# When the second layer's rotary tables, the norms' transposes and the state-space projection are issued: four changes of order in a three-block kernel

## The chip, the cores and the metric

The kernel runs on one core of one Trainium2 chip. A core has five engines that run side by side and wait for each other only by semaphores: TensorE (PE, matmuls; its weight loads are PEld), VectorE (DVE), ScalarE (ACT), GpSimd (POOL) and SyncE (SP, which here issues the transfers from memory). The metric is the device time of one execution in microseconds, the median over runs.

## What is computed

Two layers of a first block (sequence 256, width 1024, feed-forward width 4096), each with attention and pooling side by side and a feed-forward, and then a second block with a state-space branch, an attention branch and a feed-forward. All in float32. In a layer, w_in gives the columns for the pooling, for q, for k and v, and the gates; q and k are normalized per head and rotated (rope) before the attention.

```python
def hybrid_layer(x, mod, ...):
    shift1, scale1, gate1, shift2, scale2, gate2 = jnp.split(mod[:, None, :], 6, axis=-1)
    h = rms_norm(x, norm1) * (1.0 + scale1) + shift1
    proj = h @ w_in
    ...
    mix = jnp.concatenate([y_pool, y_nsa], axis=-1) @ w_out
    x = x + gate1 * mix
    h2 = rms_norm(x, norm2) * (1.0 + scale2) + shift2
    ff = jnp.square(jax.nn.relu(h2 @ w_ff1)) @ w_ff2
    return x + gate2 * ff

def second_block(x, ...):
    u = h @ w_in
    z, xbc, dt_f_raw, dt_b_raw, q, k, v, gate_logits = jnp.split(u, ...)
    y_ssd = ssd_branch(z, xbc, ...) @ w_proj_ssd
    y_att = attention_branch(q, k, v) @ w_proj_attn
    gates = jax.nn.sigmoid(gate_logits + b_gate).reshape(bsz, s, N_BRANCHES, D_MODEL)
    mix = (gates[:, :, 0] * y_ssd + gates[:, :, 1] * y_att) @ w_out
    h = layer_norm(alpha * h + mix, ln1_g, ln1_b)
    f = jnp.square(jax.nn.relu(h @ w_up)) @ w_down
    h = layer_norm(alpha * h + f, ln2_g, ln2_b)
```

## The kernel before

Every float32 product is done as three matmuls: each operand is split into a high part, rounded to a format that PE reads fast, and the low rest. For activations these are hh and hl (made by `split`: hh on ACT at L103, hl on DVE at L106), for weights wh and wl. A weight chunk (512 KB) arrives in wst by a transfer that SP issues, ACT copies it to wh (L144), DVE subtracts to get wl (L145), and PE runs its 6 to 24 matmuls at L89.

The 256 tokens are two halves, t = 0 and t = 1, of 128 rows each; x0 and x1 hold them. An RMS norm of a half (`rms`) squares and sums on ACT, forms the mean on DVE (ss, L665), takes the power -1/2 on POOL (L119), and scales on DVE (xn, L668). Then `to_fm` brings it to feature-major form: eight transposes on PE (L479, four into bank tr and four into bank pv), scale and shift (hf: L488 on DVE, L486 on ACT), and the split into hh and hl, which PE then reads. How far behind the norm the transposes are put into the program is a number of steps:

```python
later(TU["ln"], lambda: to_fm(t, xn, hi, lo, MC[l, q0 + 1], MC[l, q0]))
```

A step (`tick`) is one group of matmuls of the product that is running; `later(n, f)` calls f after n steps. `Plan.at(step, f)` puts f at a step of a layer's big projection. From the program in this order each engine gets its instructions, as far as a scheduler that looks ahead leaves them there; the order within an engine is fixed before the run.

A layer keeps rotary tables (tab, ctab: the norm's weights times cosine and sine), made by POOL. `fetch` issues the transfers of three band matrices for the pooling and four pieces of w1, and fills part of kk. The feed-forward goes through eight slices of 512 columns: up(c) into bank st, ReLU (fr, L411 on ACT; in the first two slices transposed back on PE at L416), the square (L398 on ACT, L399 on POOL, the rest frl on DVE at L400), and down(c) into the four acc banks. `between(c)` is called after down(c). After its last slice `done` starts the next norm, half by half (t = 1 first within a layer, t = 0 first into layer 1). Sums for the modulation (macc, DVE L573) are mixed in between.

In the second block `large2` runs one big projection column group by column group, its gates (sig, ACT L1439) last but one: each gate reads an acc bank. `proj_ssd` then takes the same four acc banks (ybk) for the product of the state-space output yT (yh, yl) with w_proj_ssd: per chunk k six matmuls for each bank. After w_out, `done_ln1` makes the LayerNorm of a half (xn, L1708) and its transposes.

Of the kernel before, what the change touches and what calls it, by code (L numbers as in the profile page):

```python
# [24 lines left out]
ALPHA = 2.0 ** 0.25  # L25

SZ = 1024
TU = dict(aheadq=4, nst=5, tabc=2, nw=9, nt2=23, raw=1, krest=2, qrest=4, pool2=1, c2=3, c3=1, c4=1, ln=3, uv='uv', pre=[1], nv=5, nv1=0, nv0=0, u0=19.5, du=0.7, ub=2, uc=4, c0=32.5, dc=0.1, w0=36, dw=0.5, comp=22, pool=27, dpool=2, cmpa=32, cmpb=34, dcmp=2, e1=1, e0=1, pta=2, ahead=3, modp=3, rf=0.95, r0=0, r0b=3, r1=0.8, r1b=1.2, rs=17, raw_=4, qrest_=6, u0_=19.5, du_=1.0, comp_=22, pool_=26, cmpa_=31, cmpb_=35, nv_=0, nv0_=0, w0_=32, dw_=0.8, order2='v0 qk0 qk1 qk2 v1 B C x0 z0 x1 z1 x2 z2 x3 z3 g2 g3 pa g0 g1 ps', fm0=148, dfm=9, dts=8, dcd=30, par0=10, par1=40, d0=50, dd=2, db=3, dc2=5, ss0=70, ds=5.6, scb=5, sx=3, sr=6, sg=3.5, sy=3.5, sn=8, mf0=5, modp1=99, rf1=0.5, pool2_=3, c3_=2, c4_=3, nv1_=2, dpool_=2, dcmp_=1, dc_=0.4, cap=4, ub_=2.5, c0_=32.5, pta_=4)
NST, NW = TU['nst'], TU['nw']
NT2, NT4, NS5 = TU['nt2'], 5, 20  # L30

# [30 lines left out]
def tile_two_blocks(ctx: ExitStack, tc: tile.TileContext, I, out, stop=None, dbg=None):  # L62
# [450 lines left out]
    g2 = {}  # L513
# [177 lines left out]
    def first_norm(xn, rows, hi, lo, c):  # L691
# [17 lines left out]
            V.tensor_scalar(hf[:, ks], bt[:, ks], m[:, 2 + k:3 + k], m[:, k:k + 1], op0=OP.mult, op1=OP.add)  # L709
        split(fl(hi[:, 2 * c:2 * c + 2]), fl(lo[:, 2 * c:2 * c + 2]), hf, A)  # L710

    def hybrid_layer(l, hilo, between, done):
        hi, lo = hilo
        g = lay[l]
        act = act_of(hi, lo)
        U = lambda n: TU[n + "_"] if l and n + "_" in TU else TU[n]


        tabs = {}
        tab = [t2([128, 2, 2, 2, 64], "tab") for _ in range(2)]  # L720
        ctab = s5([32, 2, 64], "ctab")

        def tables():
            for i, n in enumerate(("qn", "kns", "knw")):
                tb = tab[i // 2][:, i % 2]
                w = P(l, n)
                for t in range(2):
                    cs, sn = C("cos")[:, t * 32:(t + 1) * 32], C("sin")[:, t * 32:(t + 1) * 32]
                    for hf in range(2):
                        G.tensor_tensor(tb[:, t, 0, hf * 32:(hf + 1) * 32], w[:, hf * 32:(hf + 1) * 32], cs, op=OP.mult)  # L730
                    G.tensor_tensor(tb[:, t, 1, 32:], w[:, 0:32], sn, op=OP.mult)
                    G.tensor_tensor(tb[:, t, 1, :32], w[:, 32:64], sn, op=OP.mult)  # L732
                    G.tensor_scalar(tb[:, t, 1, :32], tb[:, t, 1, :32], -1.0, None, op0=OP.mult)
                tabs[n] = tb
            w = P(l, "kn0")[:32]
            for hf in range(2):
                G.tensor_tensor(ctab[:, 0, hf * 32:(hf + 1) * 32], w[:, hf * 32:(hf + 1) * 32], C("ccos")[:32], op=OP.mult)
            G.tensor_tensor(ctab[:, 1, 32:], w[:, 0:32], C("csin")[:32], op=OP.mult)
            G.tensor_tensor(ctab[:, 1, :32], w[:, 32:64], C("csin")[:32], op=OP.mult)
            G.tensor_scalar(ctab[:, 1, :32], ctab[:, 1, :32], -1.0, None, op0=OP.mult)  # L740
# [45 lines left out]
        def evac_k(t, ps):  # L786
            k = t2([128, 8, 64], "kS")
            A.activation(fl(k), ps, AF.Copy)
            kd = t2([128, 4, 2, 64], "kd")
            for i in range(2):  # L790
                src = ps[:, 384 * i:384 * i + 128].rearrange("p (a b) -> p a b", a=2)
                A.activation(kd[:, 2 * i:2 * i + 2], src[:, :, None, :].to_broadcast([128, 2, 2, 64]), AF.Copy)
            later(U("raw") + 2 * t, lambda: raw_kv(t, kd))
            kr, rk = head_norm(k[:, 2:6], 4)
            tmp = t2([128, 4, 64], "krt")
            for i, n in ((0, "kns"), (1, "knw")):
                rope(kr[:, 2 * i:2 * i + 2], k[:, 2 + 2 * i:4 + 2 * i], tabs[n][:, t], tmp[:, 2 * i:2 * i + 2],
                     rk[:, 2 * i:2 * i + 2], 2)
# [29 lines left out]
        def evac_q(t, ps):  # L828
            q = t2([128, 8, 64], "qS")
            A.activation(fl(q), ps, AF.Copy)  # L830
            sq, r = head_norm(q, 8)
            rqs[t] = small.tile([128, 2, 8], FT, name="rqs", bufs=2)
            V.tensor_scalar(rqs[t][:, 0], r, -0.125, None, op0=OP.mult)
            V.tensor_copy(rqs[t][:, 1], r)
            qr = t2([128, 4, 2, 64], "qr")
            tmp = t2([128, 8, 64], "qrt")
            tab = tabs["qn"][:, t]
            by_group = lambda a: a.rearrange("p (g h) d -> p h g d", g=2)
            V.tensor_tensor(qr, by_group(q), tab[:, 0][:, None, None, :].to_broadcast([128, 4, 2, 64]), op=OP.mult)
# [49 lines left out]
        def compress2(hid):  # L889
# [14 lines left out]
                for i in range(2):  # L904
                    V.tensor_tensor(krd[:, i:i + 1], o, rb, op=OP.mult)

            rope(kr, kc, ctab, sq, ss[:, 1:2], 1, last)
            hv = s5([128, 2, 4, 16], "chv")
            V.tensor_copy(hv[64:128], hid[64:128][:, :, None, :].to_broadcast([64, 2, 4, 16]))
            later(U("c3"), lambda: compress3(hv, krd))  # L910
# [188 lines left out]
        def start():  # L1099
# [4 lines left out]
            for c in range(4):  # L1104
# [15 lines left out]
                if c == TU["tabc"]:  # L1120
                    nc.sync.dma_start(cst[:, 256:], I["cst"][:, 256:])
                    load_par(0)
                    tables()
                if c == 2:
                    W.depth = TU["aheadq"]
            for n, ev in (("q", evac_q), ("k", evac_k)):
# [454 lines left out]
    def proj_ssd():  # L1581
# [120 lines left out]
    def done_ln1(t):  # L1702
# [139 lines left out]
```

## Time and profile before

| | |
|---|---|
| median of 3 runs | 1243.47 us (1239.06 to 1244.24) |
| the profiled execution's own time | 1244.79 us |
| its span | 1243.0 us |
| mean granted clock of PE | 0.984 |
| PE busy | 1188.5 us (96%) |
| DVE busy | 831.0 us (67%) |
| ACT busy | 628.9 us (51%) |
| POOL busy | 194.6 us (16%) |

The span is that of one execution taken by the profiler; the time beside it also holds what lies around it. PE is nearly always busy, so time can change where PE waits, or where its granted clock (1.00 is 2.4 GHz, 0.50 is 1.2 GHz; a mean over a stretch lies between) is under 1.00. Names as tr, xn or hl are tiles of the program; "x4" behind an instruction joins four that follow each other.

### The profile page before, as it was taken

The page shows a single profiled execution, that of the slowest core. Times are in us where ns is not written, and L with a number is a line of the kernel's source. Part 1 is how long each engine was busy: PE and PEld are TensorE (multiplying, and loading weights), DVE is VectorE, ACT ScalarE, POOL GpSimd, SP SyncE. Part 2 cuts the span into 40 slices and gives each one's busy share as a digit, 9 for nine tenths or more (in the row PEclk, how much of TensorE's full clock was granted, in tenths as well). Part 3 has the DMA queues.
Part 4 walks back from the last instruction along what each step waited for, and adds up shares of the span by engine and source line. Part 5 has one row for each costly group of instructions (what it writes and reads, how often), then busy time and mean ns, then how long its engine had stood idle before and what let it go on. Part 6 is the DMA issues. An engine that isn't in the chain of part 4 may idle for free.

```text
span 1243.0 us, 19309 instructions
## 1 busy us (share of the span) xinstructions
PE 1188.5 (96%) x7352; PEld 1023.4 (82%) x7352; DVE 831.0 (67%) x1357; ACT 628.9 (51%) x1102; POOL 194.6 (16%) x207
## 2 busy tenths in 40 slices
PE   5999999999998999999999999999999999899997
PEld 2566787999876788789988999888888898799896
DVE  2466478887767866875453745688899768744544
ACT  2335446445445654654443543567688544645440
POOL 0421011311316100121110000011122102301101
PEclk8899999999998999999999999999999999999999
DMA  8867548899877620776663556575386654666640
GB/s 283 308 228 232 179 149 286 270 321 330 271 258 249 207 78 28 255 250 191 187 187 106 183 183 222 152 204 170 102 242 218 239 167 128 211 205 185 187 135 35
DMA packets 101788, 249.21 MB, mean 200 GB/s; under 512 B 9784, under 2 KB 15036, under 8 KB 101695
## 3 DMA queue, kind: packets, MB, share of 16 engines
q1 hardware_dynamic: 100902, 247.11, 62.4%
q8 instruction: 58, 0.95, 0.3%
q10 hardware_dynamic: 792, 0.86, 0.2%
q14 instruction: 36, 0.29, 0.1%
HBM read 246.03 MB, written 1.11 MB: 199 GB/s over the span
## 4 chain that ended last, share of the span: by engine, by line
PE 60%; issue 7%; DVE 7%; DMA 5%; POOL 3%; ACT 2%; DVEq 0%; SPq 0%; ACTq 0%; POOLq 0%
PE acc L89 38%; PE st L89 16%; DMA wst<-in_w_ff_dram 3%; DVE wl L145 2%; PE pv L89 2%; PE tr L89 2%; ACT wh L144 1%; DVE macc L573 1%; DMA wst<-in_w_mod_dram 1%; POOL fr L399 1%; DMA R<-rows 1%; POOL tab L732 1%; DMA wst<-in_w_down_dram 0%; PE st L980 0%; DVE frl L400 0%
## 5 line engine op out<-in xcount | busy, mean ns | idle before, releaser
L145 DVE TENSOR_TENSOR wl<-wst,wh 128x1024 fp32r<-128x1024 f32 (+3 forms) x324 | 401.4, 1249 | 143.2 <-ACT wh L144 142.1
L144 ACT ACTIVATE wh<-wst 128x1024 fp32r<-128x1024 f32 (+3 forms) x324 | 334.8, 1048 | 280.0 <-PE acc L89 83.7
L89 PE MATMUL st<-hh,wl 128*128 128x256 f32 x576 | 163.0, 283 | 0.0
L89 PE MATMUL st<-hl,wh 128*128 128x256 f32 x576 | 163.0, 283 | 0.0
L89 PE MATMUL st<-hh,wh 128*128 128x256 f32 x576 | 163.0, 283 | 0.0
L89 PE MATMUL acc<-wh,frl 128*128 128x512 f32 x384 | 152.6, 397 | 8.3 <-DVE frl L400 8.2
L89 PE MATMUL acc<-wl,frh 128*128 128x512 f32 x384 | 151.3, 394 | 0.0
L89 PE MATMUL acc<-wh,frh 128*128 128x512 f32 x384 | 151.2, 394 | 0.0
L399 POOL TENSOR_TENSOR fr<-fr 128x512 f32<-128x512 f32 x48 | 66.0, 1375 | 402.7 <-ACT frh L398 357.6
L89 PEld LDWEIGHTS st<-hl,wh 128*128 128x128 f32 x576 | 110.5, 192 | 0.9
L89 PEld LDWEIGHTS st<-hh,wl 128*128 128x128 f32 x576 | 110.4, 192 | 0.9
L89 PEld LDWEIGHTS st<-hh,wh 128*128 128x128 f32 x576 | 110.5, 192 | 0.0
L89 PEld LDWEIGHTS acc<-wh,frl 128*128 128x128 f32 x384 | 73.2, 191 | 26.0 <-DVE frl L400 11.7
L89 PE MATMUL acc<-wh,hl 128*128 128x512 f32 (+3 forms) x224 | 89.1, 404 | 1.3 <-DVE hl L106 1.3
L89 PE MATMUL acc<-wl,hh 128*128 128x512 f32 (+3 forms) x224 | 87.6, 391 | 2.4 <-DVE wl L145 2.4
L89 PE MATMUL acc<-wh,hh 128*128 128x512 f32 (+3 forms) x224 | 87.1, 389 | 0.0
L89 PEld LDWEIGHTS acc<-wh,frh 128*128 128x128 f32 x384 | 72.9, 190 | 15.3
L89 PEld LDWEIGHTS acc<-wl,frh 128*128 128x128 f32 x384 | 73.2, 191 | 14.2
L89 PE MATMUL acc<-hh,wl 128*128 128x256 f32 x288 | 83.0, 288 | 0.4 <-DVE ym L1462 0.4
L89 PE MATMUL acc<-hl,wh 128*128 128x256 f32 x288 | 81.9, 284 | 0.0
L89 PE MATMUL acc<-hh,wh 128*128 128x256 f32 x288 | 81.4, 283 | 0.0
L573 DVE SCALAR_TENSOR_TENSOR macc<-wst,cact,macc 128x1024 f32<-128x1024 f32 x55 | 72.6, 1320 | 5.1 <-DMA wst<-in_w_mod_dram 4.9
(341 smaller groups left out, 2250.4 us busy)
## 6 DMA issues: line engine op xcount, KB each, us to landing
wst<-in_w_ff_dram SPq DMA_DIRECT2D x128, 512.0 KB, 4.5
wst<-in_w_mod_dram SPq DMA_DIRECT2D x96, 512.0 KB, 5.2
wst<-in_w_in_dram SPq DMA_DIRECT2D x76, 512.0 KB, 4.7
wst<-in_w_up_dram SPq DMA_DIRECT2D x32, 512.0 KB, 4.0
wst<-in_w_down_dram SPq DMA_DIRECT2D x32, 512.0 KB, 4.3
wst<-in_w_out_dram SPq DMA_DIRECT2D x24, 512.0 KB, 3.8
ww<-in_w_in_dram SPq DMA_DIRECT2D x16, 512.0 KB, 5.6
R<-rows SPq DMA_DIRECT2D x32, 256.0 KB, 5.7
```

The source lines that it names most:

```text
L89: T.matmul(o, l, r, start=start, stop=stop, skip_group_check=True)
L144: A.activation(h[:, :kc * n], st[:, :kc * n], AF.Copy)
L145: V.tensor_tensor(l[:, :kc * n], st[:, :kc * n], h[:, :kc * n], op=OP.subtract)
L399: G.tensor_tensor(r, r, r, op=OP.mult)
L573: V.scalar_tensor_tensor(acc, st, cact[:, k:k + 1], acc, op0=OP.mult, op1=OP.add)
L732: G.tensor_tensor(tb[:, t, 1, :32], w[:, 32:64], sn, op=OP.mult)
```

## The change

Four pieces. The tables of layer 1 are made in the feed-forward of layer 0 after down(5) instead of at the start of layer 1. `fetch` of layer 1 is put at step 5 of its plan instead of ahead of it. The transposes of the norms come 5 steps behind the norm instead of 3, and those of the second block's first LayerNorm 5 steps behind instead of at once. `proj_ssd` takes its first two chunks together: both on banks 0 and 1, then both on banks 2 and 3.

```diff
-TU = dict(aheadq=4, ... ln=3, ...)
+TU = dict(fet=5, aheadq=4, ... ln=5, ...)
...
+    rope_tables = {}
+
+    def make_tables(l):
+        tabs = {}
+        tab = [t2([128, 2, 2, 2, 64], "tab") for _ in range(2)]
+        ctab = s5([32, 2, 64], "ctab")
+        for i, n in enumerate(("qn", "kns", "knw")):
+            tb = tab[i // 2][:, i % 2]
+            w = P(l, n)
+            for t in range(2):
+                cs, sn = C("cos")[:, t * 32:(t + 1) * 32], C("sin")[:, t * 32:(t + 1) * 32]
+                for hf in range(2):
+                    G.tensor_tensor(tb[:, t, 0, hf * 32:(hf + 1) * 32], w[:, hf * 32:(hf + 1) * 32], cs, op=OP.mult)
+                G.tensor_tensor(tb[:, t, 1, 32:], w[:, 0:32], sn, op=OP.mult)
+                G.tensor_tensor(tb[:, t, 1, :32], w[:, 32:64], sn, op=OP.mult)
+                G.tensor_scalar(tb[:, t, 1, :32], tb[:, t, 1, :32], -1.0, None, op0=OP.mult)
+            tabs[n] = tb
...
+        rope_tables[l] = tabs, ctab
...
                     load_par(0)
-                    tables()
+                    make_tables(0)
...
+        plan = Plan()
         if l:
-            tables()
-            fetch()
-        plan = Plan()
+            plan.at(U("fet"), fetch)
...
     def between0(c):
         if c == 4:
             load_par(1)
+        if c == 5:
+            make_tables(1)
...
-        for k in range(12):
+
+        plan.until(("fm", 0))
+        kept = [W.next(True) for _ in range(2)]
+        for b in (0, 2):
+            for k in range(2):
+                for i in range(2):
+                    proj(kept[k], k, b + i)
+                if b:
+                    W.release(1)
+                tick()
+                yield
+        for k in range(2, 12):
             if k % 4 == 0:
                 plan.until(("fm", k // 4))
...
-        to_fm(t, xn, *hh, Q("ln1g"), Q("ln1b"))
+        later(TU["ln"], lambda: to_fm(t, xn, *hh, Q("ln1g"), Q("ln1b")))
```

The first place is POOL's order around the start of layer 1; ss is a norm's mean, fr the squares of the feed-forward, macc a modulation sum. Before, with rows of the tables left out in the middle:

```order
L566 MEMSET macc 128x1024 x3
L399 TENSOR_TENSOR fr<-fr 128x512 x4
L576 TENSOR_TENSOR macc<-macc,wst 128x1024
L119 TENSOR_TENSOR ss<-ss,half 128x1
L730 TENSOR_TENSOR tab<-par,cst 128x32 x2
L731 TENSOR_TENSOR tab<-par,cst 128x32
L732 TENSOR_TENSOR tab<-par,cst 128x32
...
L733 TENSOR_SCALAR tab<-tab 128x32 x2
L119 TENSOR_TENSOR ss<-ss,half 128x1
L119 TENSOR_TENSOR hr<-hss,half 128x8
```

After:

```order
L566 MEMSET macc 128x1024 x3
L399 TENSOR_TENSOR fr<-fr 128x512 x2
L725 TENSOR_TENSOR tab<-par,cst 128x32 x2
L726 TENSOR_TENSOR tab<-par,cst 128x32
L727 TENSOR_TENSOR tab<-par,cst 128x32
...
L728 TENSOR_SCALAR tab<-tab 128x32 x2
L399 TENSOR_TENSOR fr<-fr 128x512 x2
L576 TENSOR_TENSOR macc<-macc,wst 128x1024
L119 TENSOR_TENSOR ss<-ss,half 128x1 x2
L119 TENSOR_TENSOR hr<-hss,half 128x8
```

The thirty instructions on tab stand between the squares of two slices, and the powers of both halves' norms follow each other.

The second place is DVE's order at the start of layer 0's feed-forward, from the norm of the first of its halves to the split that PE waits for (x_91 is half 0, x_92 half 1). Before:

```order
L668 TENSOR_SCALAR xn<-x_92,ss 128x512 x2
L145 TENSOR_TENSOR wl<-wst,wh 128x1024 x2
L488 TENSOR_SCALAR hf<-tr,mcol 128x128 x4
L1072 TENSOR_TENSOR rtmp<-acc,mgate 128x512
L106 TENSOR_TENSOR hl<-hf,hh 128x4x128 x2
L1073 TENSOR_TENSOR x_91<-x_91,rtmp 128x512
L1072 TENSOR_TENSOR rtmp<-acc,mgate 128x512
L145 TENSOR_TENSOR wl<-wst,wh 128x1024
L1073 TENSOR_TENSOR x_91<-x_91,rtmp 128x512
```

After:

```order
L668 TENSOR_SCALAR xn<-x_92,ss 128x512 x2
L145 TENSOR_TENSOR wl<-wst,wh 128x1024 x2
L1074 TENSOR_TENSOR rtmp<-acc,mgate 128x512
L488 TENSOR_SCALAR hf<-tr,mcol 128x128
L1075 TENSOR_TENSOR x_91<-x_91,rtmp 128x512
L488 TENSOR_SCALAR hf<-tr,mcol 128x128 x3
L145 TENSOR_TENSOR wl<-wst,wh 128x1024
L106 TENSOR_TENSOR hl<-hf,hh 128x4x128 x2
L1074 TENSOR_TENSOR rtmp<-acc,mgate 128x512
L145 TENSOR_TENSOR wl<-wst,wh 128x1024
```

Between xn and the hl of this half there are now also an update of x and a third weight split.

The third place is PE's order in the state-space projection; acc_9439 to acc_9442 are its banks 0 to 3, wh_9315 and wl_9316 chunk 0, wh_9360 and wl_9361 chunk 1. Before:

```order
L89 MATMUL acc_9440<-yh_9260,wl_9316 128x256
L89 MATMUL acc_9440<-yl_9261,wh_9315 128x256
L89 MATMUL acc_9440<-yh_9260,wh_9315 128x256
L1568 MATMUL tr_9477<-cst_75,yg_8251 128x128 x4
L89 MATMUL acc_9439<-yh_9260,wl_9361 128x256
L89 MATMUL acc_9439<-yl_9261,wh_9360 128x256
L89 MATMUL acc_9439<-yh_9260,wh_9360 128x256
L89 MATMUL acc_9441<-yh_9260,wl_9316 128x256
L89 MATMUL acc_9441<-yl_9261,wh_9315 128x256
L89 MATMUL acc_9441<-yh_9260,wh_9315 128x256
L89 MATMUL acc_9441<-yh_9260,wl_9316 128x256
```

After:

```order
L89 MATMUL acc_9440<-yh_9260,wl_9361 128x256
L89 MATMUL acc_9440<-yl_9261,wh_9360 128x256
L89 MATMUL acc_9440<-yh_9260,wh_9360 128x256
L89 MATMUL acc_9440<-yh_9260,wl_9361 128x256
L89 MATMUL acc_9440<-yl_9261,wh_9360 128x256
L89 MATMUL acc_9440<-yh_9260,wh_9360 128x256
L1571 MATMUL tr_9477<-cst_75,yg_8251 128x128 x4
L89 MATMUL acc_9441<-yh_9260,wl_9316 128x256
L89 MATMUL acc_9441<-yl_9261,wh_9315 128x256
L89 MATMUL acc_9441<-yh_9260,wh_9315 128x256
L89 MATMUL acc_9441<-yh_9260,wl_9316 128x256
L89 MATMUL acc_9441<-yl_9261,wh_9315 128x256
```

Before, 15 matmuls stand ahead of the first one on bank 2 (twelve of chunk 0, three of chunk 1); now 24 do.

## Rows read from the trace of the kernel before

**Rows 1.** the page's part 1: busy time, share of the span and instructions

```profile
PE 1188.5 (96%) x7352; PEld 1023.4 (82%) x7352; DVE 831.0 (67%) x1357; ACT 628.9 (51%) x1102; POOL 194.6 (16%) x207
```

**Rows 2.** waits of PE: what ended them, us in total, times, longest

```profile
PE tr L479 <- DVE xn L1708: 2.5, 2, 2.1
...
PE tr L848 <- DVE qr L843: 1.5, 1, 1.5
```

**Rows 3.** timeline, start of layer 1: start, us, instruction, [idle before <- what ended it]

```profile
376.54 0.63 PE L479 MATMUL tr<-cst,xn 128*128 128x128 f32 x4 [2.96 <-DVE xn L668]
...
392.43 0.66 PE L479 MATMUL tr<-cst,xn 128*128 128x128 f32 x4 [2.78 <-DVE xn L668]
...
391.88 0.88 DVE L668 TENSOR_SCALAR xn<-x,ss 128x512 f32<-128x512 f32 x2 [2.82 <-POOL ss L119]
```

**Rows 4.** timeline of POOL, 300 to 402 us

```profile
355.78 1.04 POOL L399 TENSOR_TENSOR fr<-fr 128x512 f32<-128x512 f32 x1 [20.01 <-DMA wst<-in_w_in_dram]
...
375.85 0.64 POOL L730 TENSOR_TENSOR tab<-par,cst 128x32 f32<-128x32 f32 x2
...
376.84 0.24 POOL L732 TENSOR_TENSOR tab<-par,cst 128x32 f32<-128x32 f32 x1
...
380.02 4.26 POOL L732 TENSOR_TENSOR tab<-par,cst 128x32 f32<-128x32 f32 x1
...
391.28 0.57 POOL L119 TENSOR_TENSOR ss<-ss,half 128x1 f32<-128x1 f32 x1
```

**Rows 5.** windows: length, busy time of PE to POOL, granted clock, DMA share, GB/s

```profile
360.00:400.00 40.00, 33.46 (x141) 27.04 (x142) 30.43 (x42) 17.12 (x30) 19.90 (x33) 0.91 0.72 232
...
960.00:1000.00 40.00, 37.51 (x299) 36.83 (x298) 29.95 (x47) 23.41 (x46) 6.29 (x4) 0.96 0.67 232
```

**Rows 6.** timeline, first matmuls of the state-space projection, and its gates on ACT

```profile
972.20 0.28 PE L89 MATMUL acc<-yh,wl 128*128 128x256 f32 x1
...
973.51 0.28 PE L89 MATMUL acc<-yh,wh 128*128 128x256 f32 x1
...
977.08 0.39 PE L89 MATMUL acc<-yh,wl 128*128 128x256 f32 x1 [2.49 <-ACT sig L1439]
...
977.80 0.46 ACT L1439 ACTIVATE sig<-acc,bgh 128x256 f32<-128x256 f32 x1
```

**Rows 7.** timeline, start of the first layer's feed-forward, PE and DVE

```profile
175.79 0.60 PE L479 MATMUL tr<-cst,xn 128*128 128x128 f32 x4
...
177.13 0.39 PE L89 MATMUL acc<-wh,mh 128*128 128x512 f32 x1
...
180.76 0.40 PE L89 MATMUL st<-wh,hl 128*128 128x512 f32 x1
...
177.38 1.36 DVE L488 TENSOR_SCALAR hf<-tr,mcol 128x128 f32<-128x128 f32 x4
...
179.26 1.28 DVE L106 TENSOR_TENSOR hl<-hf,hh 128x512 fp32r<-128x512 f32 x2
```

**Rows 8.** timeline, the second layer's feed-forward, PE and DVE

```profile
496.98 1.28 DVE L106 TENSOR_TENSOR hl<-hf,hh 128x512 fp32r<-128x512 f32 x2
...
499.37 0.39 PE L89 MATMUL st<-wh,hl 128*128 128x512 f32 x1
...
521.19 1.29 DVE L573 SCALAR_TENSOR_TENSOR macc<-wst,cact,macc 128x1024 f32<-128x1024 f32 x1 [1.73 <-DMA wst<-in_w_mod_dram]
...
526.75 0.50 PE L89 MATMUL acc<-wh,frl 128*128 128x512 f32 x1 [2.38 <-DVE frl L400]
```

**Rows 9.** timeline of DVE, second half of layer 1's first norm

```profile
398.15 1.29 DVE L106 TENSOR_TENSOR hl<-hf,hh 128x512 fp32r<-128x512 f32 x2 [0.70 <-ACT hh L103]
...
402.58 0.17 DVE L833 TENSOR_SCALAR rqs<-hr 128x8 f32<-128x8 f32 x1 [1.54 <-POOL hr L119]
...
403.07 1.22 DVE L145 TENSOR_TENSOR wl<-wst,wh 128x1024 fp32r<-128x1024 f32 x1
```

**Rows 10.** the tile band, 380 to 520 us: duration min/median/max, first and last start

```profile
L89 PE MATMUL tr<-band,uS x24: 275/275/377, 443.1 to 449.6; 128*128 128x128 f32 x24
```

More of the change, by code (lines that the diff above doesn't have):

```diff
@@ L27 @@
 SZ = 1024
-TU = dict(aheadq=4, nst=5, tabc=2, nw=9, nt2=23, raw=1, krest=2, qrest=4, pool2=1, c2=3, c3=1, c4=1, ln=3, uv='uv', pre=[1], nv=5, nv1=0, nv0=0, u0=19.5, du=0.7, ub=2, uc=4, c0=32.5, dc=0.1, w0=36, dw=0.5, comp=22, pool=27, dpool=2, cmpa=32, cmpb=34, dcmp=2, e1=1, e0=1, pta=2, ahead=3, modp=3, rf=0.95, r0=0, r0b=3, r1=0.8, r1b=1.2, rs=17, raw_=4, qrest_=6, u0_=19.5, du_=1.0, comp_=22, pool_=26, cmpa_=31, cmpb_=35, nv_=0, nv0_=0, w0_=32, dw_=0.8, order2='v0 qk0 qk1 qk2 v1 B C x0 z0 x1 z1 x2 z2 x3 z3 g2 g3 pa g0 g1 ps', fm0=148, dfm=9, dts=8, dcd=30, par0=10, par1=40, d0=50, dd=2, db=3, dc2=5, ss0=70, ds=5.6, scb=5, sx=3, sr=6, sg=3.5, sy=3.5, sn=8, mf0=5, modp1=99, rf1=0.5, pool2_=3, c3_=2, c4_=3, nv1_=2, dpool_=2, dcmp_=1, dc_=0.4, cap=4, ub_=2.5, c0_=32.5, pta_=4)
+TU = dict(fet=5, aheadq=4, nst=5, tabc=2, nw=9, nt2=23, raw=1, krest=2, qrest=4, pool2=1, c2=3, c3=1, c4=1, ln=5, uv='uv', pre=[1], nv=5, nv1=0, nv0=0, u0=19.5, du=0.7, ub=2, uc=4, c0=32.5, dc=0.1, w0=36, dw=0.5, comp=22, pool=27, dpool=2, cmpa=32, cmpb=34, dcmp=2, e1=1, e0=1, pta=2, ahead=3, modp=3, rf=0.95, r0=0, r0b=3, r1=0.8, r1b=1.2, rs=17, raw_=4, qrest_=6, u0_=19.5, du_=1.0, comp_=22, pool_=26, cmpa_=31, cmpb_=35, nv_=0, nv0_=0, w0_=32, dw_=0.8, order2='v0 qk0 qk1 qk2 v1 B C x0 z0 x1 z1 x2 z2 x3 z3 g2 g3 pa g0 g1 ps', fm0=148, dfm=9, dts=8, dcd=30, par0=10, par1=40, d0=50, dd=2, db=3, dc2=5, ss0=70, ds=5.6, scb=5, sx=3, sr=6, sg=3.5, sy=3.5, sn=8, mf0=5, modp1=99, rf1=0.5, pool2_=3, c3_=2, c4_=3, nv1_=2, dpool_=2, dcmp_=1, dc_=0.4, cap=4, ub_=2.5, c0_=32.5, pta_=4)
 NST, NW = TU['nst'], TU['nw']
@@ L710, in first_norm @@
         split(fl(hi[:, 2 * c:2 * c + 2]), fl(lo[:, 2 * c:2 * c + 2]), hf, A)
+    rope_tables = {}
[14 more added lines that the diff above has]
+            tabs[n] = tb
+        w = P(l, "kn0")[:32]
+        for hf in range(2):
+            G.tensor_tensor(ctab[:, 0, hf * 32:(hf + 1) * 32], w[:, hf * 32:(hf + 1) * 32], C("ccos")[:32], op=OP.mult)
+        G.tensor_tensor(ctab[:, 1, 32:], w[:, 0:32], C("csin")[:32], op=OP.mult)
+        G.tensor_tensor(ctab[:, 1, :32], w[:, 32:64], C("csin")[:32], op=OP.mult)
+        G.tensor_scalar(ctab[:, 1, :32], ctab[:, 1, :32], -1.0, None, op0=OP.mult)
+        rope_tables[l] = tabs, ctab
     def hybrid_layer(l, hilo, between, done):
@@ L716, in hybrid_layer @@
         U = lambda n: TU[n + "_"] if l and n + "_" in TU else TU[n]
[L719 to L740, printed above, removed]
         def rope(o, x, tab, tmp, r, nh, last=None):
@@ L796, in evac_k @@
             for i, n in ((0, "kns"), (1, "knw")):
-                rope(kr[:, 2 * i:2 * i + 2], k[:, 2 + 2 * i:4 + 2 * i], tabs[n][:, t], tmp[:, 2 * i:2 * i + 2],
+                rope(kr[:, 2 * i:2 * i + 2], k[:, 2 + 2 * i:4 + 2 * i], rope_tables[l][0][n][:, t], tmp[:, 2 * i:2 * i + 2],
                      rk[:, 2 * i:2 * i + 2], 2)
@@ L836, in evac_q @@
             tmp = t2([128, 8, 64], "qrt")
-            tab = tabs["qn"][:, t]
+            tab = rope_tables[l][0]["qn"][:, t]
             by_group = lambda a: a.rearrange("p (g h) d -> p h g d", g=2)
@@ L905, in last @@
                     V.tensor_tensor(krd[:, i:i + 1], o, rb, op=OP.mult)
-            rope(kr, kc, ctab, sq, ss[:, 1:2], 1, last)
+            rope(kr, kc, rope_tables[l][1], sq, ss[:, 1:2], 1, last)
             hv = s5([128, 2, 4, 16], "chv")
```

## The prediction

> **What bounds the kernel now.** I read the page first: the matmul engine PE is busy 1188.5 us of a span of 1243.0 [rows 1], so all its idle time is 54.5 us, and no edit here takes a matmul away. The most that the change can give is therefore a part of those 54.5 us and of the time that PE spends at the lower clock. Next I read the list of PE's waits [rows 2], to see which of them the edits touch, and then the timelines around each of them. Four stretches matter.
>
> First, the start of layer 1. PE waits 2.96 us for the first token half's normalized rows and 2.78 us for the second's [rows 3]. Only the second has to do with the tables: GpSimd (POOL) makes them from 375.85 to 391.28, 15.4 us, and the reciprocal root of the second half's norm (line L119) stands behind them [rows 4]. VectorE (DVE) sits idle 2.82 us for that root before it can write xn [rows 3]. Over 360 to 400 us the granted clock is 0.91, so the two waits also cost 40 x 0.09 = 3.6 us of clock, about 1.8 each [rows 5].
>
> Second, the state-space projection: 2.49 us for a gate (sig) that still holds an accumulator bank, with a granted clock of 0.96 over 960 to 1000, which is 40 x 0.04 = 1.6 us [rows 5, 6].
>
> Third, the starts of both feed-forwards of the first block: here PE does not wait for the norm's result at all; the margin is thin [rows 7, 8]. Fourth, the LayerNorm of the second block: 2.5 us in two waits, 2.1 and 0.4 [rows 2].
>
> **The tables.** The 30 POOL instructions for layer 1 move from between the two roots to a place between the squares of the sixth and the seventh up-projection, where POOL idled 20.01 us before 355.78 [rows 4]. 15.4 us fit there with 4.6 to spare, and PE does not read a table there. So the new place costs nothing; if the cover is gone (tables longer than 20 us), each further us goes on the squares at 355.78 and from there on PE's waits for frl. They can get longer: the same operation took 0.24 us at 376.84 and 4.26 us at 380.02, beside a DVE that was nearly always busy [rows 4]. The Trainium skill speaks against the move here: the page "SBUF — State Buffer", section "SBUF: two separate sides", has GpSimd and a VectorE operation with two SBUF inputs hold one port pair as an exclusive lock for the whole instruction, and the new place is full of such VectorE splits. The 4.26 us agree with that. By the rule the new place is no better than the old one; by the row it is no worse, since the 15.4 us were already measured beside a saturated DVE.
>
> What is it worth at the old place? The root now follows ss at once, so xn is written at about 389.1 to 389.4, some 2.6 us earlier, and PE's 2.78 us and its clock loss go. But this is not PE's gain yet, since DVE's order changes with it: the second half's hf and hl, which stood directly behind three weight splits, now stand behind the rotation of q and four more instructions. Working with the durations of before: xn 389.2, its 0.9, three splits 3.5 (to 393.5); the rotation from 399.36 to 403.07, 3.7 (to 397.2), in which 1.54 us is a wait for POOL that stays; a split, qr, mcol, a split, mcol, 3.0 (to 400.2); hf 1.36; hl 1.29: 402.9 [rows 9]. Before, hl was done at 399.44. So the hidden part of the second half comes 3.5 us later while everything else on DVE is 3 us ahead; PE takes its other matmuls (some 48 of 0.227 us) in the meantime. On PE the two nearly cancel: I put the stretch itself at 0. What remains is that DVE is ahead afterwards, and the next wait of PE on DVE, 1.5 us for qr [rows 2], should go. Term: -1.5, bounds -4 (the wait, the split and the clock all go) and +2 (PE waits out hl and the clock falls again).
>
> **The transfers** of fetch (three bands, four w1 pieces) now go behind five more chunks of w_in on the queue of SP. Their first reader is at 443.1 us [rows 10], over 30 us after they are issued even so, and the w_in chunks ahead come earlier. 0; without that cover, at most one landing, some 5 us.
>
> **Transposes five steps on.** A step is a few matmuls; on PE the order below shows what it is in each place.
>
> Layer 1, first half: its transposes come 3 matmuls later than before. At 3.63/16 = 0.227 us a matmul (177.13 to 180.76) [rows 7] that covers 0.7 us of the 2.96. Term -0.7; bounds 0 and -2.5 (the clock does not fall after a 2.3 us wait).
>
> Layer 0, first half of the feed-forward: six matmuls later, 1.36 us, so at 177.15 instead of 175.79 [rows 7]. First use of the split result hl stays where it was on PE, 180.76; before, hl began at 179.26 and its first half was done at 179.9, 0.8 us early. Now DVE has in front of hl: one rtmp (0.6), an hf, an x (0.6), three hf (1.0) and one more weight split (1.15), beginning when PE's transposes allow, 178.0. That is hl from 181.5, its first half at 182.2, and PE stands 1.5 us. The other half loses another 0 to 1.2, I take 0.5. Against it, the transposes of the squared rows come two matmuls sooner, which covers 0.45 of the later wait for frl. Term +1.6, bounds -1.5 (no stall, and the frl wait short enough to keep the clock) and +2.7.
>
> Layer 1, feed-forward: five matmuls, 1.1 us; before, the first half of hl was done at 497.7 and needed at 499.37, 1.7 us of margin [rows 8]; a macc of 1.28 us is now ahead of hl on DVE, which makes a stall of about 1. But at the end of this stretch DVE waits 1.73 us for a transfer, and PE's 2.38 us for frl come behind that [rows 8]: what PE loses before, it waits less there. Term +0.5, bounds -1.5 and +1.6.
>
> Second block's LayerNorm: the first half's transposes come 18 matmuls later, four us, which covers its 0.4 us wait [rows 2]; the second half's come 3 sooner, with xn somewhat earlier. Term -0.4, bounds +1 and -1.
>
> **The projection.** Before, PE ran 15 matmuls of chunks 0 and 1 that need only banks 0 and 1, then needed bank 2. Now it runs all 24 of them first. Spacing is 1.31/11 = 0.119 us (972.20 to 973.51) [rows 6], so 9 more cover 1.1 us of 2.49. Then bank 3 is wanted 6 matmuls after bank 2, where before 10 lay between; its gate ends at 977.80 + 0.46 = 978.26 [rows 6], and PE would be there at 977.8: 0.5 of the gain comes back. That leaves 0.6, and two short waits (1.4 and 0.5) in place of a long one. With those the clock should stay up, worth the 1.6. Term -2.2, bounds -0.6 and -2.7. The second kept chunk is held for 12 matmuls longer; PE reads the next chunk at the same place in its order as before, so no load is late.
>
> **Sum:** -1.5 - 0.7 + 1.6 + 0.5 - 0.4 - 2.2 = -2.7 us. The profiled execution took 1244.79 us, 1.8 more than its span, so it would be 1242.1; that execution stands 1.3 above the median of the runs (1243.47), so for a median I say 1241. A measurement of this kernel can tell about 0.5%, 6.2 us, from no change.
>
> **Rivals.** (1) The small gain above, all in terms of one or two us: 1238 to 1244; chance 0.55. (2) The clock stays up in more places than I count: after the first wait of layer 1 (1.8) and at one or both of the frl waits of some 2.2 us (about 1.6 each over 40 us), and the second half's 2.8 us come through in full: 1241 - 1.8 - 1.6 - 2.5 = 1235. For it: these waits are only little over others here that lose nothing; against it: three of them would have to shrink. Chance 0.22. (3) The tables' place does nothing because DVE is what limits that stretch, and the projection's clock falls all the same: 1241 + 1.5 + 1.6 = 1244, no change at all. For it: DVE is busy 30.4 of the 40 us [rows 5]. Chance 0.15. (4) Slower: the later transposes leave hl late in every feed-forward. The point from which it decides is the margin of 0.8 and 1.7 us [rows 7, 8]; with a stall of 2.7, 1.6 and, at the LayerNorm, 2 us, and the clock falling in two of them (1.8 each), it costs 9.9 instead of the 1.7 in the sum: 1241 + 8.2 = 1249. Chance 0.08. The skill's lock, if the tables stretched to 25 us, is a smaller case of the same sign: 5 us on the frl waits, 1246.
>
> From these: faster by over 0.5% (under 1237.3) 0.24, within it 0.69, slower 0.07. The range takes in (1), (3) and the nearer part of (2) and (4): 1234 to 1247.
>
> **What would show it.** Right: no PE wait behind L119 near 390; POOL's tables between 335 and 352 with the squares at 355.8 not later; a wait for hl in layer 0 near 181; two waits for sig under 1.5 us with a clock near 1.00 over 960 to 1000; no wait for qr near 421. Wrong: the tables reach past 355; a clock of 0.91 again over 360 to 400 with a new wait for hl of the second half; feed-forward starts without a stall, which would add 2 us of gain.

## The result

The changed kernel takes 1252.13 us (median of 5 runs, 1251.94 to 1256.63), the kernel before beside it 1241.17 us (5 runs, 1239.02 to 1244.24): a ratio of 1.009, 95% interval 1.0068 to 1.0113. It is slower by 0.9%, where no change (1241, range 1234 to 1247) had been forecast. The profiled execution of the changed kernel took 1251.94 us, its span is 1250.1 us, 7.1 us longer than that of before.

### The profile after

The line of the page that answers to [rows 1]:

```profile
PE 1186.6 (95%) x7352; PEld 1021.1 (82%) x7352; DVE 832.1 (67%) x1357; ACT 629.0 (50%) x1102; POOL 198.7 (16%) x207
```

PE's busy time is 1.9 us shorter and the span 7.1 us longer, so PE idles 63.5 us instead of 54.5: 9 us of new waiting, and none of it is new work. The list of PE's waits says where (what ended them, us in total, times, longest):

```profile
PE st L89 <- DVE hl L106: 7.1, 5, 2.3
PE acc L89 <- DVE frl L400: 6.9, 5, 2.9
PE tr L89 <- ACT mgate L593: 5.2, 2, 3.5
PE acc L89 <- DVE wl L145: 4.8, 2, 2.7
PE acc L89 <- ACT sig L1442: 2.2, 2, 1.9
...
PE tr L479 <- DVE xn L668: 1.5, 1, 1.5
```

The waits that the change was to touch did get shorter: no row for qr and none for the LayerNorm's xn is left [rows 2]; of the 2.96 and 2.78 us at layer 1's start [rows 3] 1.50 us remain. In their place stand 7.1 us for hl, which the prediction reckoned with in part, and 5.2 us for mgate, which it doesn't name at all. Before, the view has neither row. The same waits in PE's timeline (start, length, instruction, [idle before <- what ended it]):

```profile
181.90 0.50 PE L89 MATMUL st<-wh,hl 128*128 128x512 f32 x1 [1.11 <-DVE hl L106]
...
195.35 0.50 PE L89 MATMUL st<-wh,hl 128*128 128x512 f32 x1 [0.72 <-DVE hl L106]
...
209.45 0.50 PE L89 MATMUL acc<-wh,frl 128*128 128x512 f32 x1 [1.24 <-DVE frl L400]
...
226.05 0.47 PE L89 MATMUL tr<-mal,ones_r 128*128 128x512 f32 x1 [3.47 <-ACT mgate L593]
...
325.78 0.47 PE L89 MATMUL tr<-mal,ones_r 128*128 128x512 f32 x1 [1.71 <-ACT mgate L593]
...
401.12 0.50 PE L89 MATMUL acc<-wl,hh 128*128 128x512 f32 x1 [2.74 <-DVE wl L145]
...
505.13 0.50 PE L89 MATMUL st<-wh,hl 128*128 128x512 f32 x1 [2.33 <-DVE hl L106]
...
533.33 0.50 PE L89 MATMUL acc<-wh,frl 128*128 128x512 f32 x1 [2.90 <-DVE frl L400]
```

The two halves of layer 0's feed-forward wait for hl at 181.90 and 195.35 (1.11 and 0.72, worked out as 1.5 and 0.5). The largest new wait is the one at 226.05. What is it? In `mod_part` the 1024 columns of a gate are made in two halves: two matmuls into the bank tr, then a copy into mgate on ACT (L593), for each half. There is one tr bank, so the second half's matmul waits until the first half's copy is done. ACT's timeline around it, in the changed kernel:

```profile
218.02 1.06 ACT L144 ACTIVATE wh<-wst 128x1024 fp32r<-128x1024 f32 x1 [1.13 <-DMA wst<-in_w_ff_dram]
224.36 1.06 ACT L144 ACTIVATE wh<-wst 128x1024 fp32r<-128x1024 f32 x1 [5.28 <-DMA wst<-in_w_ff_dram]
225.33 0.58 ACT L593 ACTIVATE mgate<-tr 128x512 f32<-128x512 f32 x1
226.78 0.60 ACT L593 ACTIVATE mgate<-tr 128x512 f32<-128x512 f32 x1 [0.88 <-PE tr L89]
```

And in the kernel before:

```profile
217.82 1.06 ACT L144 ACTIVATE wh<-wst 128x1024 fp32r<-128x1024 f32 x1
222.29 0.60 ACT L593 ACTIVATE mgate<-tr 128x512 f32<-128x512 f32 x1 [3.40 <-PE tr L89]
223.78 0.60 ACT L593 ACTIVATE mgate<-tr 128x512 f32<-128x512 f32 x1 [0.89 <-PE tr L89]
225.29 1.06 ACT L144 ACTIVATE wh<-wst 128x1024 fp32r<-128x1024 f32 x1 [0.91 <-DMA wst<-in_w_ff_dram]
```

Before, the copy stood ahead of the second weight rounding wh, and ACT waited for PE. Now one more rounding stands ahead of the copy. Its weight chunk lands only just before 224.36; ACT sits idle 5.28 us for it, with the copy behind it ready since PE's matmul at 221.22. PE stands at the next tr matmul until the copy at 225.33 is over. At 325.78 it is the same, 1.71 us.

### The profile page after: what moved, and what is told of

The parts are those of the page before. It is cut to its first block, busy times and chain, and to the rows that moved or that the text cites. A ratio compares the mean times of both kernels' runs of the same rounds, so it can differ in the third digit from the quotient of the medians.

```text
span 1250.1 us, 19312 instructions
## 1 busy us (share of the span) xinstructions
PE 1186.6 (95%) x7352; PEld 1021.1 (82%) x7352; DVE 832.1 (67%) x1357; ACT 629.0 (50%) x1102; POOL 198.7 (16%) x207
## 3 DMA queue, kind: packets, MB, share of 16 engines
HBM read 246.03 MB, written 1.11 MB: 198 GB/s over the span
## 4 chain that ended last, share of the span: by engine, by line
PE 50%; DVE 3%; issue 3%; POOL 1%; ACT 1%; DMA 1%; DVEq 0%; SPq 0%; POOLq 0%; ACTq 0%
PE acc L89 34%; PE st L89 12%; PE pv L89 1%; DVE wl L145 1%; PE tr L89 1%; DMA R<-rows 1%; POOL yg L1551 0%; DVE hl L106 0%; POOL fr L399 0%; PE st L1365 0%; ACT wh L144 0%; DVE frl L400 0%; POOL yss L119 0%; DVE hf L488 0%; PE tr L1490 0%
## 5 line engine op out<-in xcount | busy, mean ns | idle before, releaser
L399 POOL TENSOR_TENSOR fr<-fr 128x512 f32<-128x512 f32 x48 | 62.8, 1313 | 387.1 <-ACT frh L398 365.4
```

What stands on the lines that cost most here:

```text
L399: G.tensor_tensor(r, r, r, op=OP.mult)
```

## The experiments

Each is compared with runs of the kernel before on the same chip (29 to 35 runs, medians of 1242.0 to 1242.8); each has 12 runs itself, e1 has 6. A traced execution is one of them, and can lie some us from the median. The theory after reading the trace: the five steps cost it, by the gate copy on ACT above all. The rivals: the tables or the projection lose time (tables made beside many VectorE splits, two weight chunks kept longer); or the five steps cost it by hl, late in every feed-forward, as in rival 4 of the prediction. The letters in an expectation are its own.

**Five steps alone** (e1_ln5_only), and **everything but the five steps** (e2_no_ln):

```diff
 # e1: the kernel before with
-ln=3
+ln=5
 # e2: the changed kernel with
-ln=5
+ln=3
-        later(TU["ln"], lambda: to_fm(t, xn, *hh, Q("ln1g"), Q("ln1b")))
+        to_fm(t, xn, *hh, Q("ln1g"), Q("ln1b"))
```

> The kernel before with one number changed, ln 5 instead of 3 (transposes of the RMS norms five steps on). Theory A, the loss comes from this number: by it ACT's copy of the gate sum (mgate) gets behind a weight copy that waits for a transfer, about 5 us in two places of layer 0's feed-forward, and the split hl is late at both feed-forward starts, so 7 to 10 us slower than before, 1248 to 1251. Theory B, the loss comes from the tables or the transfers at their new places: no difference to before, within 3 us.

> The changed kernel with both changes to the transposes taken back (ln 3, and the second block's LayerNorm transposed at once): tables, transfers and projection as changed. Theory A: 1 to 4 us faster than before, with no wait for mgate and none for hl at the feed-forward starts. Theory B: 6 to 10 us slower than before, like the changed kernel.

Measured: e1 1253.89 us, ratio 1.0101 [1.0073, 1.0129]; e2 1239.42 us, 0.999 [0.9965, 1.0014]. e1 is above the 1248 to 1251 expected by theory A. The one number from 3 to 5 is the whole slowdown (e1's LayerNorm keeps its old place). So it is not the tables, the transfers or the projection.

**The projection alone** (e3_proj_only): the kernel before with the diff's new piece of `proj_ssd` and nothing else.

> The kernel before with only the projection's pairs of banks. By the prediction 2 us faster (two short waits for sig and a full clock in place of 2.5 us and a clock of 0.96 over 40 us). The rival, read off the changed kernel's trace where the waits for sig still add to 2.2 us: no difference, within 1 us.

Measured: 1240.85 us, 0.9977 [0.995, 1.0005]. No loss, and no gain that can be told from none.

**The gate copy on DVE** (e4_gate_dve), in the changed kernel; the same values are copied by another engine:

```diff
-                A.activation(gt[:, n * 512:(n + 1) * 512], b, AF.Copy)
+                V.tensor_copy(gt[:, n * 512:(n + 1) * 512], b)
```

> The changed kernel with the copy of the gate sums out of bank tr (line L593) made by DVE instead of ACT, so that it can't stand behind a weight copy on ACT. If the queue on ACT is what costs, the two waits of 3.5 and 1.7 us for mgate go and the time is 3 to 5 us under the changed kernel, 1247 to 1249. If those waits only stand where PE would have waited anyway, for the weights that come by the same late transfers, it stays at 1251 to 1253.

Measured: 1245.96 us, 1.003 [1.001, 1.005]; 6 us less than the changed kernel. Its waits for mgate are 0.50 and 2.20 us, where the changed kernel has 3.47 and 1.71: the first nearly goes, the second does not. So the copy's place is the larger part of the slowdown, and 3 us (1.2 to 6.2) are something else.

**Five steps in one place at a time** (e5 to e7), in the kernel before; e8 is the changed kernel without the LayerNorm's shift and with five steps at layer 1's start alone:

```diff
-        later(TU["ln"], lambda: to_fm(t, xn, hi, lo, MC[l, q0 + 1], MC[l, q0]))
+        later(5 if (l, q0) == (0, 3) else 3, lambda: to_fm(...))   # e5; e6: (1, 3); e7, e8: (1, 0)
```

> The kernel before with 5 steps instead of 3 only for the norm in front of layer 0's feed-forward. If the number does its harm through the order on ACT (the gate sums behind one more weight copy, which by the order is so with this site alone), 5 to 7 us slower than before, with both waits for mgate. If it is the late hl alone, 1 to 2 us slower. If what costs is the sum of all sites, about a third of 11 us.

> The kernel before with 5 steps only for the norm in front of layer 1's feed-forward. From the changed kernel's trace, where PE waits 2.3 us for hl and then 2.9 for frl there: 3 to 4 us slower. If the later wait for frl takes the stall up, as the prediction had it: 0 to 1 us slower.

> The kernel before with 5 steps only for the norm at the start of layer 1. From the changed kernel's trace this site gives back about 1 us (the first wait 1.5 instead of 3.0, against new short waits for hl, wl and macc in the second half): between 2 us faster and 1 us slower. If the site does harm like the others, 3 us or more slower.

> Tables, transfers and projection as changed, 5 steps only at the start of layer 1, 3 elsewhere, the second block's LayerNorm transposed at once. If the sites add up: the run with no change to the transposes (1239.4) and what the site at layer 1 gives, 1237 to 1240. If the earlier tables and the later transposes get in each other's way on DVE, 1241 or more.

Measured: e5 (layer 0's feed-forward) 1248.6 us, 1.0047 [1.0029, 1.0065]; e6 (layer 1's feed-forward) 1241.6, 0.9996 [0.9973, 1.0019]; e7 (layer 1's start) 1244.8, 1.0022 [1.0, 1.0044]; e8 1242.39, 0.9998 [0.9977, 1.0019]. One place, the first, has most of it: 6.6 us; layer 1's start has 2.8, at the edge of what can be told; layer 1's feed-forward nothing, though PE waits 1.02 us for hl in it. e8 is above its first expectation, 3.0 us over e2 by the medians, as e7 is 2.8 over before, both within the intervals. In PE's timeline e7's layer-1 start, at the transposes of the second half, reads:

```profile
396.82 0.66 PE L479 MATMUL tr<-cst,xn 128*128 128x128 f32 x4 [1.23 <-DVE mcol L650]
...
399.75 0.79 PE L89 MATMUL acc<-wl,hh 128*128 128x512 f32 x1 [2.04 <-DVE wl L145]
```

The 2.96 us wait for xn of the first half is gone there, and 1.31 us remain for the second (at 389.03); PE now waits for DVE's weight split and for its columns (mcol, read out of the one tr bank). Over 352 to 412 us PE's granted clock is 0.89, where before it is 0.94. That DVE sets the pace in this place is read off these waits; no run gives DVE less to do there.

**Is it the gate copy in the first place?** e9_ff0_gate_dve is e5 with the copy on DVE as in e4.

> The kernel before with 5 steps for layer 0's feed-forward norm alone, and the copy of the gate sums on DVE instead of ACT. That site alone measured 6.6 us slower. If it is the gate's place in ACT's queue: 4 to 6 of them go, 1242 to 1245, and what stays is the late hl (1.1 and 0.4 us). If the late hl and its clock are the larger part: 1246 or more.

Measured: 1240.75 us, 0.9994 [0.9969, 1.0019]. e9 is not slower than before, and under the 1242 to 1245 expected, with the copies of L593 (six, of 0.6 us each) moved to another engine. PE's timeline of e5, the first hl wait, the frl wait and the two gate waits:

```profile
181.09 0.50 PE L89 MATMUL st<-wh,hl 128*128 128x512 f32 x1 [1.11 <-DVE hl L106]
...
209.75 0.80 PE L89 MATMUL acc<-wh,frl 128*128 128x512 f32 x1 [2.84 <-DVE frl L400]
...
227.48 0.47 PE L89 MATMUL tr<-mal,ones_r 128*128 128x512 f32 x1 [1.85 <-ACT mgate L593]
...
327.02 0.47 PE L89 MATMUL tr<-mal,ones_r 128*128 128x512 f32 x1 [1.51 <-ACT mgate L593]
```

ACT's timeline of e5 has the order of the changed kernel, the rounding that waits and then the copy:

```profile
225.79 1.06 ACT L144 ACTIVATE wh<-wst 128x1024 fp32r<-128x1024 f32 x1 [6.55 <-DMA wst<-in_w_ff_dram]
226.76 0.58 ACT L593 ACTIVATE mgate<-tr 128x512 f32<-128x512 f32 x1
```

And the rows of e9 that answer to them:

```profile
180.23 0.50 PE L89 MATMUL st<-wh,hl 128*128 128x512 f32 x1 [1.10 <-DVE hl L106]
...
207.56 0.50 PE L89 MATMUL acc<-wh,frl 128*128 128x512 f32 x1 [1.90 <-DVE frl L400]
...
319.97 0.47 PE L89 MATMUL tr<-mal,ones_r 128*128 128x512 f32 x1 [0.47 <-DVE mgate L593]
```

In e9 PE still waits for hl (1.10 us at 180.23, 0.56 at 193.52), and the kernel is not slower; 1.7 us are less than its interval (3.8 us less to 2.4 more) can tell. From the first row to the last, e5 takes 145.93 us and e9 139.74: 6.2 us are gained in the place itself. But e9 moves more than one copy. DVE's order changes with it at layer 1's start too, and of e5's waits for xn there (2.34 and 4.14 us) 1.31 is left, with 1.60 for wh and 1.01 for wl instead. What the move is worth without the shift is told by e16 below.

**Tables alone** (e10_tables_only: make_tables(1) after down(5), nothing else), **the LayerNorm's shift alone** (e11_ln1_only: five steps at the LayerNorm), and **three steps in layer 0's feed-forward alone** (e12_after_ff0_3: the changed kernel with `5 if (l, q0) != (0, 3) else 3`):

> The kernel before with only layer 1's tables made in layer 0's feed-forward. The prediction's terms for the stretch come to 1.5 us faster, with the second wait for xn gone or short. If DVE is what limits that stretch: within 1 us of before. If the tables delay the squares behind them at their new place: slower, with POOL's squares after 355 us.

> The kernel before with only the second block's LayerNorm transposed 5 steps on. By the prediction 0.4 us faster; by the changed kernel's trace, where waits for hl of 2.0 and 1.0 us take the place of those for xn, no difference, within 1 us. Harm like the other sites: 3 us or more slower.

> The changed kernel with 3 steps in front of layer 0's feed-forward alone, all else as changed. If that site is most of the loss: 6 to 7 us under the changed kernel, 1244 to 1246. If the sites work together (layer 1's feed-forward cost 3 us in the changed kernel and nothing with its own 5 steps alone): up to 9 us under it, 1243.

Measured: e10 1241.12 us, 0.9985 [0.997, 1.0001]; e11 1242.81, 1.0006 [0.9981, 1.0031]; e12 1245.98, 1.0042 [1.0017, 1.0067]. Layer 1's start in e10, on PE:

```profile
375.14 0.63 PE L479 MATMUL tr<-cst,xn 128*128 128x128 f32 x4 [2.54 <-DVE xn L668]
388.66 0.66 PE L479 MATMUL tr<-cst,xn 128*128 128x128 f32 x4 [1.98 <-DVE xn L668]
...
418.08 0.63 PE L850 MATMUL tr<-cst,qr 128*128 128x128 f32 x4 [1.50 <-DVE qr L845]
```

With the tables away the second half's wait is 1.98 instead of 2.78 us. But e6 and e11, with the tables at the old place, wait 1.88 for it, and in e6 DVE sits idle only 0.96 us for the root that took 2.82 in the trace of before. So this wait differs by as much from execution to execution, and no gain from the tables shows in it. And the wait for qr is still 1.50 us. e11 takes away the two waits for xn and has two for hl instead:

```profile
1048.70 0.50 PE L89 MATMUL st<-wh,hl 128*128 128x512 f32 x1 [1.97 <-DVE hl L106]
...
1063.64 0.50 PE L89 MATMUL st<-wh,hl 128*128 128x512 f32 x1 [0.76 <-DVE hl L106]
```

2.7 us of new waits for 2.5 of old ones, and no difference in time. e12 still stands 3.4 us over before (2.1 to 8.3), without the gate's wait: with e4 it says that 3 us or more are in layer 1.

**What is left, and whose it is** (e13 to e16). All have the gate copy on DVE. e13 is the changed kernel with three steps at layer 1's start, e15 with three at layer 1's feed-forward, e14 with three at both, e16 is e2 with the copy moved.

```diff
+        later(5 if (l, q0) != (1, 0) else 3, lambda: to_fm(...))   # e13
+        later(5 if (l, q0) == (0, 3) else 3, lambda: to_fm(...))   # e14
+        later(5 if (l, q0) != (1, 3) else 3, lambda: to_fm(...))   # e15
```

> The changed kernel with both gate copies on DVE, as in the run before that took 1246, and three steps again at layer 1's start alone (five at both feed-forwards). Theory A: what is left of the slowdown, 3.7 us, is layer 1's start, which alone cost 2.8: then 1242 to 1243 or less, with FF1 at no cost. Theory B: it is the second feed-forward in company of the first, where the stage from 489 to 677 us took 2.9 us longer than before: then still 1245 to 1246.

> The same with five steps at layer 0's feed-forward and at the LayerNorm alone (three at layer 1's start and its feed-forward). Both theories: the tables, the projection and a shift that costs nothing once the gate is off ACT, so 1238 to 1241, and the stage from 489 to 677 us within 1 us of before. If this is 1245, the shift at layer 0 harms in company whatever ACT does.

> The same with five steps at layer 0's feed-forward and at layer 1's start, three at layer 1's feed-forward. Theory A: 1246, as with all three. Theory B: 1242 to 1243, and the stage from 489 to 677 us within 1 us of before.

> The changed kernel with three steps everywhere (LayerNorm at once), so tables, transfers and projection alone, and the gate copies on DVE besides. If the gate copy waits on ACT only where five steps put it there, this is the 1239 of the same kernel with the copy on ACT, give or take 2; if the copies on ACT cost something before the change too (ACT waits 0.9 and 3.4 us around them), it is 1236 or less, and the first version here that beats the kernel before.

Measured: e13 1242.77 us, 1.0003 [0.9983, 1.0024]; e14 1240.74, 0.9997 [0.9979, 1.0014]; e15 1241.3, 0.9988 [0.9967, 1.0009]; e16 1239.2, 0.9989 [0.9968, 1.001]. Each theory (the one place or the other) holds for one of e13 and e15 and misses the other: to take either of the two away takes the remaining cost away, as far as these intervals tell. It needs both.

e14 and e16 say what e9 could not say alone. Without the shift, moving the copies changes nothing (e16 1239.2, e2 1239.42). With the copies on DVE, five steps at layer 0's feed-forward and at the LayerNorm cost 1.5 us (e14 against e16, not to be told from none), where with the copies on ACT the first of these cost 6.6 alone. The place itself shows it in every trace: the time in us from PE's first matmul on hl there (180.76 in before) to its first matmul for the second half of the second gate (320.43), in the profiled execution:

| copies | three steps there | five steps there |
|---|---|---|
| on ACT | 136.9 to 137.6 (e2, e3, e6, e7, e8, e10, e11, e12), 139.7 (before) | 143.9 (changed), 145.4 (e1), 145.9 (e5) |
| on DVE | 139.7 (e16) | 138.8 to 141.4 (e4, e9, e13, e14, e15) |

For layer 1 the traces agree too: DVE's timeline of e4 (five steps in both) ahead of the split of layer 1's feed-forward,

```profile
496.62 1.05 DVE L488 TENSOR_SCALAR hf<-tr,mcol 128x128 f32<-128x128 f32 x3
499.40 1.28 DVE L573 SCALAR_TENSOR_TENSOR macc<-wst,cact,macc 128x1024 f32<-128x1024 f32 x1 [1.73 <-DMA wst<-in_w_mod_dram]
500.60 1.29 DVE L106 TENSOR_TENSOR hl<-hf,hh 128x512 fp32r<-128x512 f32 x2
```

and that of e13 (five in the feed-forward, three at layer 1's start):

```profile
492.73 1.04 DVE L488 TENSOR_SCALAR hf<-tr,mcol 128x128 f32<-128x128 f32 x3
493.69 1.21 DVE L145 TENSOR_TENSOR wl<-wst,wh 128x1024 fp32r<-128x1024 f32 x1
494.98 1.29 DVE L106 TENSOR_TENSOR hl<-hf,hh 128x512 fp32r<-128x512 f32 x2
```

With the shift at layer 1's start, a modulation sum that waits 1.73 us for its transfer comes to stand in front of hl, and PE waits 2.53 us for hl there; without it a weight split that waits for nothing stands there, and PE waits 1.02. The sum stands there in the four kernels with both shifts (the changed one, e1, e4, e12), and not in e6, e13 and e15. That this is what costs there is read from the traces; no run moves the sum alone, and why it is due there only then was not tried.

## Why the prediction was wrong

**The step that failed** is "Layer 0, first half of the feed-forward", +1.6 with bounds of -1.5 and +2.7; e5 measures 6.6 (0.29% to 0.65%, 3.6 to 8.1 us). Its reckoning of hl held: late by 1.11 and 0.72 us for 1.5 and 0.5. The shorter wait for frl that it set against this is not shown: 1.24 us in the changed kernel and 2.17 in the trace of before (at 208.49), but 2.84 in e5, and 0.71 to 1.86 in the eight other kernels with three steps and the copy on ACT. What was missing is an engine. The step asked "how late are PE and DVE", and never looked at what the shift moves on ACT, 40 us further on: a rounding that waits 5.28 us for its transfer ahead of a 0.58 us copy that holds the only tr bank. With that copy off ACT's queue the shift costs 1.5 us (e14 against e16, with the LayerNorm's) instead of 6.6. In the trace of the changed kernel the two waits for the gate are 5.2 us. In e5's own they are 3.4 of the 6.3 us that the place takes more than in the trace of before; 1.1 more are the waits for frl and the second half's hl, and the clock, 0.91 over 40 us from 207.48 where before has 0.96, can account for the remaining 1.8 (40 x 0.05 = 2).

**Layer 1, first half**: -0.7 (0 to -2.5) was forecast, e7 measures +2.8 (0 to 5.5). The 2.96 us wait for xn did go, but the step took PE's wait as the thing to cover. In e7 PE waits for DVE again right behind it, 1.31 for the second half's xn, 1.23 for a modulation column and 2.04 for a weight split, and at a lower clock.

**Layer 1, feed-forward**: +0.5 was right for the shift alone (e6: -0.4). With the shift at layer 1's start beside it hl comes behind a waiting sum. The sum of terms took the places as independent; they are not.

**The tables**: -1.5 was forecast. e10's 0.9985 [0.997, 1.0001] is -1.9 us with an interval that ends at none: right as far as it can be told, but not for its reasons: the second xn wait is 1.98 us, no shorter than in kernels with the tables at the old place (1.88 in e6 and e11), and the qr wait did not go with the tables alone. That the first trace showed 2.78 there, and 4.26 us for one operation on a table, was of that execution (the longest in e6, at the same place, is 1.26). The new place was dearer than worked out; POOL after:

```profile
339.18 1.88 POOL L725 TENSOR_TENSOR tab<-par,cst 128x32 f32<-128x32 f32 x2
...
358.96 0.54 POOL L728 TENSOR_SCALAR tab<-tab 128x32 f32<-128x32 f32 x2
359.45 1.04 POOL L399 TENSOR_TENSOR fr<-fr 128x512 f32<-128x512 f32 x1
```

The 30 instructions took 20.3 us, 15.4 at the old place [rows 4], and filled the gap to its end: the squares at 359.45 start behind the last of them without a pause. PE's two waits for frl that follow are 0.91 and 0.92 us, so nothing is lost. The Trainium skill, "SBUF — State Buffer", section "SBUF: two separate sides", states an exclusive lock on the port pair that GpSimd shares with VectorE operations on two SBUF inputs, as the splits are. The 4.9 us more agree with it, though no run here separates the lock from other causes. The forecast that the tables end by 352 fails, even if the some 4 us are taken off by which the changed kernel is behind at this point.

**The transfers**: 0, and no row after shows a wait for them. They were never moved alone.

**The LayerNorm**: -0.4 (within 1 each way); e11 gives 0.7 us more, with an interval from 2.4 less to 3.9 more, so none.

**The projection**: -2.2 (-0.6 to -2.7). The nine matmuls more cover 1.1 us as worked out: PE stands at bank 2 3.5 us after its first matmul, 2.4 before. But its gate ends later too, and the waits are 1.95 and 0.26 us, 2.2 together for the 2.49 of before. The clock is the larger part of the term, and in the changed kernel it stays at 0.96. Two windows of it, for [rows 5] (length, busy PE to POOL, granted clock, DMA share, GB/s):

```profile
360.00:400.00 40.00, 33.87 (x157) 26.48 (x155) 31.44 (x44) 18.74 (x32) 9.09 (x6) 1.00 0.72 219
960.00:1000.00 40.00, 37.79 (x296) 36.59 (x296) 30.69 (x46) 26.30 (x54) 5.38 (x4) 0.96 0.73 243
```

At layer 1's start the fall of the clock is later, not gone: over 395 to 435 us, around the 2.74 us wait for wl, it is 0.91. The window of e2's projection, where the first wait is 1.71 us:

```profile
952.00:992.00 40.00, 38.02 (x312) 37.10 (x312) 31.47 (x48) 24.17 (x46) 5.50 (x4) 1.00 0.73 240
```

There the clock stays at 1.00, and from the start of the second block to the end of the projection e2 is 1.9 us shorter than before (1.8 in e4, whose clock is 1.00 too). In the changed kernel this stretch is 0.1 us longer than before. So the term was of the right size where the clock stayed up, and nothing where it fell; the prediction took the first for certain. Over 40 us placed alike in the profiled executions, the clock is 1.00 in seven of the ten kernels with the new order (not in the changed one, e3 and e16) and in one of the eight with the old (e9). e3, the projection alone, measures 2.9 us less than before by its ratio, from 6.2 less to 0.6 more.

**The rivals.** "Slower" was rival 4, with hl late in every feed-forward and 1249 us. hl is late in all three places (1.83, 2.33 and 2.97 us, with 2.7, 1.6 and 2 reckoned), and the sign was its own; but e6, e9 and e11 have these waits one at a time and are no slower than their intervals of 2 to 4 us can tell. In e11 they take the place of waits for xn. That a later wait for frl gives them back, as the prediction had it, is not shown: it is 2.66 us in e6, where before has 2.38, e11 2.54 and e3 3.04. So the sign came by another way than the rival names: none of the four had ACT in it.

**The sum by the runs**: 6.6 (layer 0) + 2.8 (layer 1's start) - 0.4 (its feed-forward) = 9.0; e1, all three at once, has 11.1; the 2 us between lie within the intervals, and are also what the pair in layer 1 would add. Less what tables, transfers and projection give (e2 and e16, 0.1% under before, not to be told from none) this is the 11.0 us of the changed kernel as far as it can be told. None of the sixteen kernels is faster than the one before by more than can be measured; the lowest ratio is e3's, 0.9977 [0.995, 1.0005].

## What to carry to other kernels

A number that shifts "how many steps later" moves instructions on every in-order engine, and not only in the place that it names: read the new order of each engine for a short instruction that frees a single buffer and now stands behind one that waits for a transfer. A wait that PE shows is not a gain to be had until the engine that it waits for has slack; before pricing it, look at what PE waits for next on that engine. Read it in more than one execution, too: the 2.78 us of before are 1.88 in two kernels with the same order there. Terms of places that share an order can't be added without asking what the first shift moves into the second.

## What the runs showed of the hardware

The length of a wait alone does not say whether the granted clock falls behind it. Over 40 us around PE's 3.47 us wait in the changed kernel the clock is 1.00,

```profile
206.05:246.05 40.00, 35.28 (x202) 30.65 (x201) 31.23 (x26) 20.72 (x29) 14.05 (x11) 1.00 0.78 262
```

and over 40 us from the same point of e5, around waits of 2.84 and 1.85 us, it is 0.91,

```profile
207.48:247.48 40.00, 35.88 (x192) 31.32 (x193) 29.88 (x26) 18.67 (x26) 14.17 (x11) 0.91 0.68 232
```

while the changed kernel's 1.95 us wait in the projection goes with 0.96, and e9's 2.34 us wait in the same place with 1.00. A term for the clock has to keep both ends; it was not settled what decides it.

On POOL the same small operation with 128x32 operands took from 0.24 us (349.78) to 1.30 us (354.37) within 5 us of each other, and the thirty together a third more than at another place.
